# Hybrid decoder layer on one core: the sums of the down weights are issued from the second run of gate and up rows on

## The chip, the cores and the metric

The kernel runs on one core of one Trainium2 chip. The metric is the device time of one execution in microseconds (us). A core has five engines that run side by side, each with its own queue in a fixed order: TensorE (PE, matrix products; its weight loads are listed as PEld), VectorE (DVE), ScalarE (ACT), GpSimd (POOL) and SyncE (SP, which only issues transfers here). An instruction at the head of a queue that waits for something holds up everything behind it on that engine. Transfers are issued from SP, ACT and POOL and are carried by 16 DMA engines.

## The reference

One decoder layer on x (2048 x 1024, float32). Its first product is `proj = rms_norm(x, g) @ w_in`, split into u (512 columns, for the state-space branch), q, k and v. u goes through a diagonal state-space scan, a GELU and a gated product; q, k, v go through rotary embedding and attention over a window of 128 with sinks. Both branches are normed, joined and multiplied with w_out, normed and added to x. Then a SwiGLU feed-forward part follows: `gu = rms_norm(h) @ w_gate_up`, `ff = (silu(gate) * up) @ w_down` (2816 inner columns), normed and added.

```
def rms_norm(x, g):
    xf = x.astype(jnp.float32)
    y = xf * lax.rsqrt(jnp.mean(xf * xf, axis=-1, keepdims=True) + NORM_EPS)
    return (y * g.astype(jnp.float32)).astype(x.dtype)
```

## The kernel before, in words

Every float32 operand of a product is split into a high and a low part (line 166: a cast on ACT, a subtraction on DVE), and a product is three matmuls (lines 219 to 221). The 2048 rows are dealt with in four blocks of 512.

The first stage, `phase_proj`, weaves `u_stream` (the u products) with `table_stream` (tables for the state-space branch, mostly DVE work), and then the q, k, v products with the state-space scan. In `u_stream` the rows are not normed before the product. The product of a block is formed in four PSUM banks; beside it, x is loaded a second time in row layout (the tile `xn`, 512 KB each, four per block, two buffers), and ACT squares and sums it (`x_square`, line 344, into `ssq_x`). `rstd_block` then computes 1/sqrt for the block on POOL: `rsqrt`, lines 87 to 99, a chain of 15 tiny instructions on 128 x 4 numbers, each reading the one before. ACT writes the result into a diagonal matrix (`diag`, line 358), PE multiplies that with ones (`ps_bc`, line 360), ACT copies it out (`rstd_bc`, line 361), and DVE multiplies the block's four banks with it on their way out (`ust`, line 368). All four banks of one block have to be emptied that way before the next block's products can have them: `u_out` and the products of the next block both use the bank tag "pd", which has four.

The order of the instructions on each engine is not that of the program text. Up to the end of `phase_mix` a planner lays it out ahead of time: it goes through the program with its own reckoning of when each instruction's inputs are there and how long it will take, and gives an engine that it believes free the most urgent instruction that it believes ready. What it lays down is fixed in the queue; the chip follows that order whatever the real times are. The feed-forward part, `phase_ffn` (line 1355), stands under `manual_schedule`: there each engine keeps the order in which the program text issues its instructions. But that order only says which of them follows which. The first instruction of that part on an engine can still be laid down by the planner as early as its inputs are there, among the work of the earlier stages, and then the second one, until one comes whose input is made late.

In the feed-forward part `ffn_gu` (lines 1362 to 1399) runs over 21 runs of gate and up rows (`gu_runs`: run 0 holds rows 0 and 11, every further run one row block), each run in four quarters q. Between the products it does side work: `side` (the second half's channel transposes, q of 0 and 1), `pieces`, and `sums`. `sums` is `down_sums` (lines 1463 to 1478): 48 transfers from DRAM to DRAM, issued on POOL, that build four sums of halves of w_down in the DRAM tiles `ws_d` (`wsd` in the profile); the first 12 are plain copies out of w_down into two of the four. Each needs at most transfers issued 6 or 12 places before it. One is issued at q = 2, one at q = 3, and one at the end of each run (line 1395), so three a run, until the 48 are used up. At the end of every second run `ff_operands` (line 1448) issues three stores of the finished activations on POOL (`fxd`), which wait for DVE. `ffn_down` later reads `wsd` through SP.

Of the kernel before, what the change touches and what calls it, by code (L numbers as in the profile page):

```python
# [47 lines left out]
class Layer:  # L48
# [1313 lines left out]
    def ffn_gu(self, s):  # L1362
        nc, tc = self.nc, self.tc
        with ExitStack() as c:
            def right(name, bufs):
                return c.enter_context(tc.tile_pool(name=name, bufs=bufs, side="right", reuse_waits="tile"))

            ev, self.f_p[5] = right("f_ev", 1), right("f_p5", 1)
            ff, fc, self.f_p[6] = right("f_ff", 1), right("f_c", 1), right("f_p6", 1)
            pieces = self.act_steps(s, (5, 6), self.f_s, ("sa", "sa"))  # L1370
            pieces = [lambda: None] + pieces[:2] + [lambda: None] + pieces[2:]
            self.dn, self.dn_next = {}, 0
            sums = iter(()) if s else self.down_sums()
            side = [] if s else self.channel_steps(1, fc, "hx", 1, fc, "oo", 1, "pd")
            F4 = None
            for n, fs in enumerate(self.gu_runs()):
                if fs[0] < NJ:
                    j = fs[0]
                    F4 = ff.tile([P, 4, TB], F32, tag="f4", name=f"f4_{s}_{j}")
                groups = [self.gu_group(s, f, F4, ev) for f in fs]  # L1380
                for q in range(4):
                    for g in groups:
                        self.gu_ahead()
                        if fs[-1] == NF - 1 and q:
                            self.dn_ahead(s, q if q > 1 else 1)
                        next(g, None)
                        if pieces:
                            pieces.pop(0)()
                    if q > 1:
                        next(sums, None)  # L1390
                    elif side and n > 0:
                        side.pop(0)()
                if fs[-1] >= NJ:
                    self.ff_operands(s, j, F4)
                next(sums, None)
            for f in side:
                f()
            for _ in sums:
                pass
# [294 lines left out]
```

## Time and profile before

| | |
|---|---|
| time, median of 3 runs | 2166.42 us (2161.72 to 2170.81) |
| the profiled execution's own time | 2160.93 us |
| its span, first to last instruction | 2159.2 us |
| mean granted TensorE clock | 0.969 |
| busy: PE / DVE / ACT / POOL | 2001.8 / 1377.6 / 919.0 / 330.0 us |
| transfers from w_down or wsd into wsd | 48, of 512 KB or 256 KB |

Stages on PE by their first instruction in the trace: u products from 6.1 us, q, k and v products from 164.3, feed-forward products from 845.6 us, first read of `wsd` at 1323.3 us. A row of the timeline gives the start, the duration, the engine, the line, the operation and tiles, the number of instructions merged, and in brackets how long the engine stood idle before it and what ended that.

### The profile page before, as it was taken

How to read it: one execution, taken by the hardware profiler on the slowest of the kernel's cores; microseconds unless marked ns; L12 is line 12 of the kernel's file. 1: busy time of each engine (PE TensorE's matmuls, PEld its weight loads, DVE VectorE, ACT ScalarE, POOL GpSimd, SP SyncE). 2: the span in 40 equal slices, each digit the busy share in tenths (PEclk: the TensorE clock that was granted, in tenths of full speed). 3: DMA queues.
4: the chain of work that ended last, by engine and by line, in shares of the span. 5: the costliest groups of instructions: out<-in, count | busy, mean ns of one | idle time of the engine just before them, and what ended most of it. 6: DMA issues, size and time to landing. Idle time of an engine off the chain costs nothing.

```text
span 2159.2 us, 26000 instructions
## 1 busy us (share of the span) xinstructions
PE 2001.8 (93%) x9264; PEld 1630.3 (76%) x9264; DVE 1377.6 (64%) x2167; ACT 919.0 (43%) x1502; POOL 330.0 (15%) x667
## 2 busy tenths in 40 slices
PE   5499989889899889999999999999999999999995
PEld 3487656678787767788888888887788888888884
DVE  6548767698677676665566665557655565555447
ACT  5234211686576554533333334543433333334432
POOL 1301100021313342222122110005000000000003
PEclk8699999999999999999999999999999999999997
DMA  8246765733515683668588367766423232256655
GB/s 283 95 171 230 246 173 159 181 94 98 166 59 179 217 299 124 214 196 219 183 235 220 118 214 235 229 223 245 160 83 118 93 127 93 85 175 209 197 189 204
DMA packets 178003, 379.75 MB, mean 176 GB/s; under 512 B 32928, under 2 KB 53920, under 8 KB 177680
## 3 DMA queue, kind: packets, MB, share of 16 engines
q1 hardware_dynamic: 138400, 258.84, 37.5%
q0 software_dynamic: 32800, 110.84, 16.3%
q10 hardware_dynamic: 6672, 8.40, 1.2%
q8 instruction: 73, 1.20, 0.2%
q14 instruction: 58, 0.48, 0.1%
HBM read 281.87 MB, written 119.21 MB: 186 GB/s over the span
## 4 chain that ended last, share of the span: by engine, by line
PE 67%; DVE 8%; DMA 6%; issue 6%; POOL 3%; ACT 2%; SPq 0%; ACTq 0%; DVEq 0%; POOLq 0%
PE ps_gb L219 7%; PE ps_gb L220 7%; PE ps_gb L221 7%; PE ps_dn L220 6%; PE ps_dn L221 6%; PE ps_dn L219 6%; PE ps_gc L221 3%; PE ps_gc L219 3%; PE ps_gc L220 3%; PE ps_wo L219 2%; PE ps_wo L221 2%; PE ps_wo L220 2%; PE ps_ga L221 2%; PE ps_ga L219 2%; PE ps_ga L220 2%
## 5 line engine op out<-in xcount | busy, mean ns | idle before, releaser
L219 PE MATMUL ps_gb<-bh,wh 128*128 128x512 f32 x704 | 276.8, 393 | 6.4 <-ACT q L1420 6.1
L220 PE MATMUL ps_gb<-bl,wh 128*128 128x512 f32 x704 | 275.9, 392 | 0.0
L221 PE MATMUL ps_gb<-bh,wl 128*128 128x512 f32 x704 | 275.6, 391 | 0.0
L221 PE MATMUL ps_dn<-wh_w,wl_x 128*128 128x512 f32 x616 | 241.1, 391 | 4.4 <-DVE wl_x L171 4.4
L219 PE MATMUL ps_dn<-wh_w,wh_x 128*128 128x512 f32 x616 | 240.9, 391 | 0.6 <-ACT wh_x L170 0.5
L220 PE MATMUL ps_dn<-wl_w,wh_x 128*128 128x512 f32 x616 | 240.9, 391 | 0.0
L1330 ACT CAST wh<-gur 128x1024 fp32r<-128x1024 f32 x132 | 119.0, 902 | 182.8 <-DVE gur L75 175.1
L171 DVE TENSOR_TENSOR wl_x<-xr,wh_x 128x1024 fp32r<-128x1024 f32 x72 | 83.8, 1164 | 150.4 <-ACT wh_x L170 150.3
L75 DVE TENSOR_TENSOR wl<-gur,wh 128x1024 fp32r<-128x1024 f32 x132 | 139.5, 1057 | 50.6 <-ACT wh L1330 50.6
L219 PEld LDWEIGHTS ps_gb<-bh,wh 128*128 128x128 f32 x704 | 132.4, 188 | 37.8 <-ACT q L1420 7.7
L221 PEld LDWEIGHTS ps_gb<-bh,wl 128*128 128x128 f32 x704 | 132.4, 188 | 29.3
L220 PEld LDWEIGHTS ps_gb<-bl,wh 128*128 128x128 f32 x704 | 132.4, 188 | 28.9
L170 ACT CAST wh_x<-xr 128x1024 fp32r<-128x1024 f32 x72 | 70.8, 984 | 192.5 <-PE ps_dn L220 103.4
L220 PE MATMUL ps_gc<-bl,wh 128*128 128x512 f32 x352 | 137.9, 392 | 1.0 <-DVE bl L171 1.0
L221 PEld LDWEIGHTS ps_dn<-wh_w,wl_x 128*128 128x128 f32 x616 | 116.4, 189 | 29.4 <-DVE wl_x L171 5.3
L221 PE MATMUL ps_gc<-bh,wl 128*128 128x512 f32 x352 | 137.8, 392 | 0.0
L219 PE MATMUL ps_gc<-bh,wh 128*128 128x512 f32 x352 | 137.8, 392 | 0.0
L219 PEld LDWEIGHTS ps_dn<-wh_w,wh_x 128*128 128x128 f32 x616 | 116.4, 189 | 25.8 <-ACT wh_x L170 1.4
L220 PEld LDWEIGHTS ps_dn<-wl_w,wh_x 128*128 128x128 f32 x616 | 116.2, 189 | 24.1
L171 DVE TENSOR_TENSOR wl_w<-wr,wh_w 128x1024 fp32r<-128x1024 f32 x84 | 99.4, 1183 | 8.2 <-ACT wh_w L170 8.2
L1455 POOL DMA_DIRECT2D fxd<-f x22 | 17.1, 776 | 507.7 <-DVE f L75 463.9
L1428 ACT COPY u<-ps_gb 128x512 f32<-128x512 f32 x44 | 25.8, 587 | 142.1 <-PE ps_gb L221 142.1
(388 smaller groups left out, 4567.8 us busy)
## 6 DMA issues: line engine op xcount, KB each, us to landing
gur<-in_w_gu SPq DMA_DIRECT2D x88, 512.0 KB
xr<-fxd SPq DMA_DIRECT2D x70, 512.0 KB
wr<-wsd SPq DMA_DIRECT2D x40, 512.0 KB
fxd<-f POOLq DMA_DIRECT2D x22, 768.0 KB, 4.3
gwr_o<-in_w_out SPq DMA_DIRECT2D x64, 256.0 KB
wsd<-in_w_down POOLq DMA_DIRECT2D x30, 512.0 KB, 9.9
wr<-in_w_down SPq DMA_DIRECT2D x30, 512.0 KB
raw<-in_xT SPq DMA_DIRECT2D x56, 256.0 KB
```

Source lines behind the costliest of these rows:

```text
L75: (eng or self.nc.vector).tensor_tensor(out=out, in0=a, in1=b, op=op)
L170: nc.scalar.copy(hi, x)
L171: nc.vector.tensor_tensor(out=lo, in0=x, in1=f32(hi), op=ALU.subtract)
L219: t.matmul(out, wh, mh, start=first, stop=False, skip_group_check=more)
L220: t.matmul(out, wh, ml, start=False, stop=False, skip_group_check=more)
L221: t.matmul(out, wl, mh, start=False, stop=last, skip_group_check=more)
L1330: nc.scalar.copy(a[0], a[2])
L1428: nc.scalar.copy(u2, b)
L1455: nc.gpsimd.dma_start(to[0:3].rearrange("b p t -> p b t"), F4[:, 0:3])
```

## The change

In the first run (n = 0) the transfers at q = 2 and q = 3 are no longer issued. The one at the end of run 0 (line 1395) stays and is now the first; every later transfer moves two places back in the order in which the sums are issued. The number of transfers and what they move stay the same. With three a run and one in run 0, the last two of the 48 are now issued in run 16 instead of run 15.

```
                     if q > 1:
-                        next(sums, None)
+                        if n:
+                            next(sums, None)
                     elif side and n > 0:
                         side.pop(0)()
```

## Rows read from the trace of the kernel before

**Rows 1.** The page, busy tenths of PE in 40 equal slices of the span

```profile
PE   5499989889899889999999999999999999999995
```

**Rows 2.** Waits, 0 to 110 us: engine, tile, line, releaser, total us, times, longest

```profile
PE ps_bc L360 <- ACT diag L358: 43.9, 1, 43.9
...
POOL rsq_vd L87 <- ACT xn L344: 57.8, 4, 19.6
```

**Rows 3.** Timeline of POOL, 0 to 85 us, in the order of its queue

```profile
1.97 0.77 POOL L1477 DMA_DIRECT2D wsd<-in_w_down  x1
22.34 0.33 POOL L87 TENSOR_SCALAR rsq_vd<-ssq_x 128x4 f32<-128x4 f32 x1 [19.60 <-ACT xn L344]
34.96 0.20 POOL L87 TENSOR_SCALAR rsq_vd<-ssq_x 128x4 f32<-128x4 f32 x1 [12.29 <-ACT xn L344]
35.22 0.61 POOL L422 DMA_DIRECT2D cosd<-t_cs  x1
35.87 0.71 POOL L88 TENSOR_SCALAR rsq_hd<-rsq_vd 128x4 f32<-128x4 f32 x1
...
54.11 0.19 POOL L87 TENSOR_SCALAR rsq_vd<-ssq_x 128x4 f32<-128x4 f32 x1 [13.26 <-ACT xn L344]
...
69.38 0.61 POOL L87 TENSOR_SCALAR rsq_vd<-ssq_x 128x4 f32<-128x4 f32 x1 [12.67 <-ACT xn L344]
70.06 0.65 POOL L1477 DMA_DIRECT2D wsd<-in_w_down  x1
...
79.03 0.88 POOL L99 TENSOR_TENSOR rstd<-rsq_td,rsq_yd 128x4 f32<-128x4 f32 x2
...
81.18 0.35 POOL L92 TENSOR_TENSOR rsq_td<-rsq_yd 128x4 f32<-128x4 f32 x2
```

**Rows 4.** Timeline of all engines, 36 to 90 us

```profile
36.59 0.63 PE L221 MATMUL ps_u<-xs,wl 128*128 128x512 f32 x1
...
79.79 1.28 ACT L358 ACTIVATE diag<-ident,rstd 128x128 f32<-128x128 f32 x4 [10.49 <-POOL rstd L99]
...
81.12 2.07 PE L360 MATMUL ps_bc<-diag,ones 128*128 128x512 f32 x2 [43.91 <-ACT diag L358]
...
87.43 0.78 PE L219 MATMUL ps_u<-xs,wh 128*128 128x512 f32 x1
```

**Rows 5.** Stretches: us, busy of PE, PEld, DVE, ACT, POOL, PEclk, DMA, GB/s

```profile
0.00:37.00 37.00, 26.98 (x96) 19.41 (x96) 29.07 (x133) 22.42 (x38) 4.42 (x14) 0.96 0.85 290
37.00:81.00 44.00, 0.21 (x1) 0.00 (x0) 27.65 (x65) 15.26 (x30) 17.54 (x50) 0.54 0.58 196
81.00:92.00 11.00, 10.88 (x35) 8.88 (x36) 5.76 (x9) 2.42 (x7) 4.00 (x25) 0.51 0.00 0
92.00:155.00 63.00, 63.00 (x303) 51.72 (x302) 24.92 (x45) 18.91 (x43) 2.97 (x5) 1.00 0.36 130
155.00:400.00 245.00, 214.28 (x1044) 159.89 (x1043) 175.14 (x338) 70.95 (x162) 24.26 (x57) 0.97 0.67 200
```

**Rows 6.** Timeline of POOL, 872 to 880 us: one chain of 15, first and last

```profile
872.90 0.99 POOL L87 TENSOR_SCALAR rsq_vq<-ssq_h 128x4 f32<-128x4 f32 x1 [0.51 <-ACT junk_m L1066]
...
878.38 0.20 POOL L99 TENSOR_TENSOR rstd<-rsq_tq,rsq_yq 128x4 f32<-128x4 f32 x1
```

**Rows 7.** Timeline of POOL, 860 to 1500 us: first store of activations, last sums

```profile
893.32 0.85 POOL L1455 DMA_DIRECT2D fxd<-f  x1 [14.74 <-DVE f L75]
...
1167.72 3.63 POOL L1477 DMA_DIRECT2D wsd<-in_w_down  x4
```

**Rows 8.** Instructions that touch wsd: duration ns min/median/max, first and last start

```profile
L1223 SPq DMA_DIRECT2D wr<-wsd x48: 332/360/378, 1323.3 to 2081.5; - x48
```

**Rows 9.** Groups of DVE, 200 to 400 us: busy us, mean ns, idle before

```profile
L75 DVE TENSOR_TENSOR a<-ps_S,tab 128x512 f32<-128x512 f32 x32 | 21.2, 686 | 19.7 <-PE ps_S L654 19.7
L75 DVE TENSOR_TENSOR b<-z,tab 128x512 f32<-128x512 f32 x32 | 20.7, 688 | 0.3
L667 DVE TENSOR_TENSOR_SCAN z<-rho,a 128x256 f32<-128x256 f32 x32 | 20.3, 676 | 0.0
```

## The prediction

> **What bounds the kernel now.** I read the page's slices first. PE is busy nine tenths or more nearly everywhere, and the hole is at the start: 5 and 4 tenths in the first two slices of 54 us [rows 1]. So a change counts where it makes PE start sooner or wait less, and the first 108 us are where PE has most to gain. The waits of that stretch name the hole: one single wait of 43.9 us, of `ps_bc` for ACT's `diag` [rows 2]. The timeline shows its two ends: PE ends the first block's products at 36.59 + 0.63 = 37.22 us and starts `ps_bc` at 81.12 [rows 4]. ACT's `diag` started at 79.79, released by POOL's `rstd` [rows 4], so the cause lies on POOL.
>
> POOL's own queue tells the rest [rows 3]. The chain of the first block starts at 22.34, when that block's squares are summed. Its second step (line 88) needs nothing but the first, yet runs at 35.87. In front of it in the queue stands the first step of the second block's chain, which waits 12.29 us for that block's squares. Later the third block's first step holds POOL for 13.26 us and the fourth's for 12.67. Only then, behind a transfer into `wsd` at 70.06, does the first block's chain go on, to end at 79.03 + 0.88 = 79.91. The three foreign waits make 38.2 us of its 57.6 us. PE's hole is thus an order on POOL that doesn't fit the real times.
>
> Why that order? The two transfers into `wsd` at 1.97 and 70.06 belong to the feed-forward part; they are the two that run 0 issues at q = 2 and q = 3, laid down this early because they need nothing. On the chip POOL spends 0.77 and 0.65 us on them [rows 3]. The planner must have reckoned with far more. The second one needs nothing either and POOL stood idle for 19.60, 12.29, 13.26 and 12.67 us before it, yet it was laid down behind all four first steps. That fits only if the planner believed POOL to be occupied by the first transfer until the inputs of both the first and the second chain were there (in truth 12.6 us apart), then gave POOL the backlog most urgent first, and put in the second transfer when it saw nothing ready. `cosd` supports it, an unrelated store that went out right behind the second chain's first step. This is an inference from the order; no row states what the planner believed.
>
> **What the change does, step by step.** (a) The two transfers leave the start. The first POOL instruction of the feed-forward part is now the store `fxd`, which waits for DVE and runs at 893.32 [rows 7]; nothing of that part can be laid down on POOL before its input is made. The planner then lays out POOL's first 100 us without the two. I expect the first chain to go down in one piece, behind its own squares and before the second chain's first step.
>
> (b) The new end of the hole. The chain starts at 22.34 as now. Undisturbed, 15 steps took from 872.90 to 878.58, 5.7 us [rows 6]; beside a busy DVE the last pair of steps took 0.88 us and the undisturbed pair 0.35 [rows 3], so up to 2.5 times as long, 14.3 us. `rstd` is ready between 28.0 and 36.6. From 79.91 to `ps_bc` at 81.12 it was 1.2 us. That makes 29 to 38 us, and PE is busy with the first block until 37.2. So nearly the whole wait of 43.9 us can go: minus 43.1 to minus 43.9. I take 43.9.
>
> The Trainium skill, "SBUF — State Buffer", section "Who interferes with whom", says that a DVE instruction with two SBUF inputs and a GpSimd instruction that reads SBUF exclude each other for a whole instruction. The pairs of 0.88 and 0.35 us agree with that in direction. If each of the 15 steps lost one 0.69 us DVE instruction, the chain would take 16 us and end at 38.4, and the gain would be 41.5 in place of 43.9. The sum below doesn't use this.
>
> (c) What is late next. The queues of PE and ACT are in order too. If the planner believes the chain shorter than it is, it lays `diag` and `ps_bc` among the last products and casts of the first block, and these wait. Price: from none to the chain's full length, 14 us; the undisturbed chain's half is the nearest guess, plus 3.
>
> (d) The clock. After the hole the granted clock was 0.51 for 11 us [rows 5], near the lower level of 1.2 GHz; 35 matmuls took 10.88 us there and 303 took 63.0 afterwards, so 0.31 against 0.21 us each, 3.6 us lost. It was falling already before the hole, with PE poorly fed. Between none and minus 3.6; I take minus 1.8.
>
> (e) The loads of the start. One 512 KB transfer less while the DMA engines are 0.85 busy at 290 GB/s [rows 5]: 0.52 MB / 290 GB/s is up to 1.8 us; loads here partly wait for buffers, so minus 0.5. At 70.06 nothing on PE waited for data.
>
> (f) Given back later. DVE did 27.65 us of work under the hole [rows 5], mostly tables. It now lies beside the next blocks' products, where DVE is busy 24.92 of 63 us: 38 us are free, room for all. Behind that, 155 to 400 us, PE is busy 214 and DVE 175 of 245 [rows 5], and the order is laid out anew there as well. If all of the tables' work came onto the path, plus 27.7; if the new order closed all of PE's gaps, minus 30.7. The cover I see is nearly enough, so I take plus 5.
>
> (g) The feed-forward part. Each sum moves two places on POOL. The last four started at 1167.72 to 1171 [rows 7]; two of them go into the next run, some 20 us later. The first read of `wsd` is at 1323.3 [rows 8], so over 130 us cover it, and the stores between them move by at most two issues of about 1 us. Nothing; without that cover each late sum would hold PE about as long as a transfer takes.
>
> Sum: minus 43.9, plus 3, minus 1.8, minus 0.5, plus 5, is minus 38.2 us. The profiled execution took 2160.93 us (span 2159.2 and 1.7 around it), so 2122.7 on its scale. The median of the runs is 2166.42, 5.5 above that execution; on that scale 2128.2, and I predict 2128. From the start of the u products' second block on all is bound by PE and by order, nothing by absolute time, so what is won there should reach the end.
>
> **Rivals.** (1) The order stays as it is: the planner had another reason to lay the first steps ahead, for instance that it believes the squares of all blocks to come close together. Then only the transfers' own time goes: 0.65 us off the chain and up to 1.8 of (e), so 2164 to 2166. For it: the pair of chains at 81.18 also runs in lockstep [rows 3]. Against it: the second transfer's place, which that does not explain.
>
> (2) The hole goes and about half is given back in the state-space stage: DVE holds the a, z and b steps there, 62.2 us of busy time with 19.7 us of waits for PE [rows 9], and tables that come later than u would stretch it. Terms (c) and (f) at 14 and 12 then leave about minus 20: 2146.
>
> (3) Slower than before. The planner, with u early, lays the q products ahead of the state-space products, because the tables can't come sooner. The a, z, b steps then no longer lie beside q products. Place: 200 to 400 us. Price: up to 62.2 us uncovered [rows 9] plus the 14 of (c), against a gain of about 46 from (b), (d) and (e); it decides from 46 us on, and the whole of it gives 2166.4 - 46 + 76 = 2196. For it: DVE is at 175 of 245 us there. Against it: the u products of three more blocks take over 60 us first, time for the tables.
>
> **How the numbers follow.** The forecast (25 to 50 us gained, 2116 to 2141) has 0.68, rival 2 0.12, rival 1 0.11, rival 3 0.09. About 0.5% (11 us) is what a measurement of this kernel can tell from no change. Faster by more than that: the forecast and nearly all of rival 2, 0.79. Within it: rival 1 and a rest, 0.12. Slower: rival 3, 0.09. Low end: terms (b), (d), (e) in full, 49 us, and 10 of the 30.7 that a better order could win in (f): 2108. High end: rival 2 with a little more given back, 2158, short of rivals 1 and 3, which hold 0.2.
>
> **What would show it.** In the profile after: no `wsd` row on POOL before the first `fxd`; POOL's first chain without a foreign wait inside, ending before 40 us; `ps_bc` before 45 us with a wait under 10 us; the second slice of PE at 8 or 9 tenths; the feed-forward part starting about 38 us earlier; its length unchanged. (f) is wrong if the stretch from the last u product to the first gate product is longer than before by more than 10 us. The prediction fails if `ps_bc` still waits for the fourth block's squares.

## The result, and the profile after

The changed kernel takes 2127.17 us (median of 4 runs, 2126.79 to 2128.03), the kernel before beside it 2164.76 (4 runs). The ratio is 0.9824, 95% interval 0.9801 to 0.9846: 37.6 us less, against 38.2 predicted. The profiled execution took 2126.79 us with a span of 2124.9, 34.3 less than the span before. In the repeat further down the gain is 40.8 us (2127.76 against 2168.56 of 9 runs of the kernel before). So the 38.2 is met within some 3 us, and the closer agreement here is luck.

The hole at the start is gone. The page of the changed kernel, busy tenths of PE, beside [rows 1]:

```profile
PE   7999798999898899999999999998999999999995
```

The cause is to be seen on POOL's queue (timeline of the changed kernel, 0 to 80 us, beside [rows 3]):

```profile
22.26 0.32 POOL L87 TENSOR_SCALAR rsq_vd<-ssq_x 128x4 f32<-128x4 f32 x1 [20.21 <-ACT xn L344]
22.66 0.25 POOL L88 TENSOR_SCALAR rsq_hd<-rsq_vd 128x4 f32<-128x4 f32 x1
...
27.52 0.20 POOL L99 TENSOR_TENSOR rstd<-rsq_td,rsq_yd 128x4 f32<-128x4 f32 x1
...
28.53 0.56 POOL L422 DMA_DIRECT2D cosd<-t_cs  x1
...
36.45 0.19 POOL L87 TENSOR_SCALAR rsq_vd<-ssq_x 128x4 f32<-128x4 f32 x1 [4.86 <-ACT xn L344]
...
57.15 0.19 POOL L87 TENSOR_SCALAR rsq_vd<-ssq_x 128x4 f32<-128x4 f32 x1
```

There is no `wsd` row left (the first is at 863.1). The second step of the first chain, at 22.66, stands right behind the first; before, the second block's first step stood between them. `rstd` is ready at 27.72 in place of 79.91. The waits of 0 to 110 us (columns as in [rows 2]) and the first `ps_bc`:

```profile
ACT diag L358 <- POOL rstd L99: 16.2, 4, 7.1
...
PE ps_u L219 <- ACT xs L170: 11.7, 4, 6.0
...
PE ps_bc L360 <- ACT diag L358: 0.2, 1, 0.2
```

```profile
29.08 1.13 PE L360 MATMUL ps_bc<-diag,ones 128*128 128x512 f32 x2 [0.20 <-ACT diag L358]
```

So 43.9 us of wait became 0.2. Where the rest of the time stands is read by stages. The last u product starts at 164.0 us before and at 125.8 after, the last score product (`ps_sc`) at 702.2 and 664.2, the first gate product (`ps_gb`) at 845.6 and 812.7. The stretches (columns as in [rows 5]), of the kernel before:

```profile
37.00:164.00 127.00, 83.09 (x376) 68.07 (x376) 64.65 (x127) 41.11 (x91) 26.86 (x83) 0.80 0.44 153
164.00:702.20 538.20, 484.64 (x2582) 389.78 (x2581) 397.79 (x762) 281.05 (x572) 87.29 (x220) 0.97 0.54 158
702.20:845.60 143.40, 127.75 (x607) 104.21 (x606) 94.13 (x142) 74.35 (x122) 48.78 (x108) 0.95 0.68 226
```

of the changed kernel:

```profile
0.00:37.00 37.00, 26.97 (x102) 19.64 (x102) 29.84 (x126) 22.92 (x41) 9.41 (x34) 1.00 0.81 276
37.00:125.80 88.80, 83.34 (x371) 67.53 (x371) 61.79 (x134) 38.74 (x89) 22.83 (x60) 0.92 0.64 212
125.80:664.20 538.40, 484.90 (x2582) 391.22 (x2580) 398.49 (x762) 281.30 (x571) 87.46 (x220) 0.96 0.53 158
664.20:812.70 148.50, 132.97 (x608) 108.75 (x607) 94.52 (x142) 74.49 (x122) 49.30 (x108) 0.92 0.65 218
```

The u stage gained 38.2 us (164.0 to 125.8). The state-space and score stages took the same, 538.2 and 538.4. The stretch behind them took 5.1 more, the feed-forward part 1.4 less (1313.6 and 1312.2). The sum is minus 34.3.

### The profile page after: what moved, and what is told of

The parts are those of the page before. It is cut to its first block, busy times and chain, and to the rows that moved or that the text cites. A ratio compares the mean times of both kernels' runs of the same rounds, so it can differ in the third digit from the quotient of the medians.

```text
span 2124.9 us, 25992 instructions
## 1 busy us (share of the span) xinstructions
PE 2006.2 (94%) x9264; PEld 1635.4 (77%) x9264; DVE 1375.8 (65%) x2167; ACT 917.6 (43%) x1502; POOL 331.9 (16%) x667
## 4 chain that ended last, share of the span: by engine, by line
PE 69%; DVE 8%; issue 6%; DMA 5%; POOL 3%; ACT 2%; SPq 0%; ACTq 0%; DVEq 0%; POOLq 0%
PE ps_gb L219 7%; PE ps_gb L220 7%; PE ps_gb L221 7%; PE ps_dn L221 6%; PE ps_dn L219 6%; PE ps_dn L220 6%; PE ps_gc L221 4%; PE ps_gc L220 4%; PE ps_gc L219 4%; PE ps_wo L219 2%; PE ps_wo L221 2%; PE ps_wo L220 2%; PE ps_ga L220 2%; PE ps_ga L219 2%; PE ps_ga L221 2%
```

## The experiments

The theory: the two early transfers cost through the place that they push the first reciprocal-root chain to, and the planner does that because it believes a transfer to hold the issuing engine for long. The rivals: the transfers cost by themselves (POOL's time, load on the DMA engines); only the second one, ahead of the chain's rest, does the harm; any early instruction does it, whatever it moves.

**One transfer left at the start.**

```diff
-                        if n:
+                        if n or q == 2:
                             next(sums, None)
```

> The changed kernel, but of the two transfers of run 0 the first (at q = 2) is issued there again; only the second stays away. Nothing of the computation is left out. Order theory (the transfers cost through the place that they push the first block's reciprocal-root chain to, not through their own time): one transfer at the head of POOL's queue is enough to split the first chain, so ps_bc again waits about 43 us for diag, and the time is 2160 to 2166. Rival, transfers that cost by themselves, each the same: half of the 37.6 us comes back, about 2146, with a wait of about 22 us. Rival, only the second transfer (the one at 70.06 ahead of the chain's rest) does the harm: about 2127, and no wait above 10 us.

Measured 2166.34 us (10 runs) against 2167.44 of before, ratio 0.9999 (0.9989 to 1.0009). One transfer does all of the harm, and it is the first. POOL's timeline shows the split of before, with no second `wsd`:

```profile
1.98 0.76 POOL L1478 DMA_DIRECT2D wsd<-in_w_down  x1
21.87 0.22 POOL L87 TENSOR_SCALAR rsq_vd<-ssq_x 128x4 f32<-128x4 f32 x1 [19.14 <-ACT xn L344]
35.47 0.28 POOL L87 TENSOR_SCALAR rsq_vd<-ssq_x 128x4 f32<-128x4 f32 x1 [13.38 <-ACT xn L344]
...
53.81 0.19 POOL L87 TENSOR_SCALAR rsq_vd<-ssq_x 128x4 f32<-128x4 f32 x1 [13.08 <-ACT xn L344]
...
68.64 0.19 POOL L87 TENSOR_SCALAR rsq_vd<-ssq_x 128x4 f32<-128x4 f32 x1 [12.23 <-ACT xn L344]
```

```profile
78.68 2.07 PE L360 MATMUL ps_bc<-diag,ones 128*128 128x512 f32 x2 [42.90 <-ACT diag L358]
```

**Both transfers kept, the chains on DVE.**

```diff
-        self.rsqrt(self.rstd1[:, sl], self.ssq_x[:, sl], D, 4)
+        self.rsqrt(self.rstd1[:, sl], self.ssq_x[:, sl], D, 4, eng=nc.vector)
```

> The kernel before, with both transfers at POOL's start as they were, but the reciprocal-root chains of the input's rows (rstd1) computed on DVE in place of POOL. Nothing of the computation is left out. Order theory: what the transfers hold up on POOL is no longer on the path, so the wait of 43.9 us goes with the transfers still there: 2122 to 2135. Rival, the transfers' own cost (their 1.4 us on POOL, their load on the DMA engines at the start, or anything else that goes with their being early): the time stays at 2160 to 2167. Rival, the chain on DVE gets behind the tables there: the wait is shortened in part only, 2140 to 2155.

Measured 2127.61 us, ratio 0.9821 (0.9798 to 0.9843): the whole gain with both transfers where they were. The first rows are POOL's, the last is PE's, which waits for nothing there:

```profile
1.97 0.75 POOL L1477 DMA_DIRECT2D wsd<-in_w_down  x1
...
70.51 0.57 POOL L1477 DMA_DIRECT2D wsd<-in_w_down  x1
```

```profile
37.12 1.02 PE L360 MATMUL ps_bc<-diag,ones 128*128 128x512 f32 x2
```

The same chains on DVE without the two early transfers took 2126.31 us (further down). So neither the DMA load of the early transfers nor their time on POOL cost anything that can be measured. It was what stood behind them in POOL's queue.

**The transfers early on ACT's queue.**

```diff
         L.setup()
+        for jp in range(2):
+            tc.nc.scalar.dma_start(L.ws_d[1][jp][0:2],
+                                   I["w_down"][2 * jp:2 * jp + 2, :, 512:1024])
...
+                if dst == S1 and op is None and jp < 2:
+                    continue
```

> The changed kernel, but the two transfers that it took from the start are issued there all the same, from ACT's queue right behind the setup, so that the DMA engines carry the same 1 MB early and POOL carries none of it. The sum is the same. Order theory: POOL's first chain stays in one piece, ps_bc starts before 40 us, and the time is that of the changed kernel, 2126 to 2133 (up to 2 us for the DMA time and two issues on ACT). Rival, the early load is what cost the time: 2155 to 2166.

A miss: 2168.01 us (10 runs), ratio 1.0006 (0.9988 to 1.0024), just above the 2155 to 2166 that the load rival gave. But the trace shows another cause. Rows of DVE and of PE:

```profile
51.13 1.29 DVE L171 TENSOR_TENSOR xs<-raw,xs 128x512 fp32r<-128x512 f32 x2
```

```profile
13.43 0.80 PE L219 MATMUL ps_u<-xs,wh 128*128 128x512 f32 x1 [13.43 <-ACT wh L173]
51.87 0.79 PE L220 MATMUL ps_u<-xs,wh 128*128 128x512 f32 x1 [37.65 <-DVE xs L171]
```

DVE's very first `xs` was laid behind its table steps and ran at 51.13, though ACT's cast for it began at 5.80 and took 0.62 us; in the changed kernel the first one ran at 6.15. With no `xs` done, no buffer came free: SP waited 38.5 us for it with the next loads, and the DMA engines were 0.05 busy from 17 to 50 us. So the transfers made a hole of like size (37.65 us) in another place. That is how the theory's mechanism would look with ACT as the engine believed to be held. As a test of the load this kernel was no good, since it changed the order as well. The kernel above is the test of the load, and the one with small pieces on ACT tests this reading.

**Smaller pieces at POOL's start.** The kernel before, but each of the first two sums moves 8 of its 128 rows, in the second kernel 32; the rest of both follows with the third sum.

```diff
+        late = []
...
+                if dst == S1 and op is None and jp < 2:
+                    late.append((y[:, 8:], x[:, 8:]))
+                    y, x = y[:, 0:8], x[:, 0:8]
+                else:
+                    while late:
+                        nc.gpsimd.dma_start(*late.pop(0))
```

> The kernel before, with both sums issued in run 0 as there, but each of these two first moves only 8 of its 128 rows (32 KB in place of 512); the rest of both follows with the third sum. The sums are the same. The theory that the planner lays POOL's queue out by the length that it believes a transfer to have: two short ones don't hold POOL in its plan, so the first chain stays whole, ps_bc waits under 1 us, and the time is that of the changed kernel, 2125 to 2131, though the two transfers still stand at the head of POOL's queue. Rival, any transfer that is free to go at the start splits the chain: the hole of about 43 us stays, 2160 to 2167.

> As the kernel with 8 rows, but 32 of the 128 rows of each (128 KB). Place theory: the queue then has the second block's first step in front of the first block's second, and the fourth block's first step in front of the first chain's end, so a quarter of the bytes costs the whole hole: ps_bc again waits about 43 us, 2160 to 2167. Rival, cost in proportion to the bytes moved early: a quarter of 37.6 us, about 2137.

With 8 rows 2127.52 us, ratio 0.9818 (0.9794 to 0.9841); with 32 rows 2160.47, ratio 0.9958 (0.9942 to 0.9974). POOL's timeline with 8 rows:

```profile
1.97 1.40 POOL L1484 DMA_DIRECT2D wsd<-in_w_down  x2
21.52 0.44 POOL L87 TENSOR_SCALAR rsq_vd<-ssq_x 128x4 f32<-128x4 f32 x1 [18.14 <-ACT xn L344]
22.04 0.66 POOL L88 TENSOR_SCALAR rsq_hd<-rsq_vd 128x4 f32<-128x4 f32 x1
...
27.66 0.24 POOL L99 TENSOR_TENSOR rstd<-rsq_td,rsq_yd 128x4 f32<-128x4 f32 x1
```

and with 32:

```profile
1.97 0.89 POOL L1484 DMA_DIRECT2D wsd<-in_w_down  x1
22.81 0.19 POOL L87 TENSOR_SCALAR rsq_vd<-ssq_x 128x4 f32<-128x4 f32 x1 [19.95 <-ACT xn L344]
35.85 0.19 POOL L87 TENSOR_SCALAR rsq_vd<-ssq_x 128x4 f32<-128x4 f32 x1 [12.85 <-ACT xn L344]
...
43.84 1.74 POOL L1484 DMA_DIRECT2D wsd<-in_w_down  x1
...
74.44 0.75 POOL L99 TENSOR_TENSOR rstd<-rsq_td,rsq_yd 128x4 f32<-128x4 f32 x2
```

At the head of the queue the real issue takes POOL 0.70, 0.89 and 0.77 us with 8, 32 and 128 rows, nearly the same. Yet the first size leaves the chain whole and the other two split it. Against the kernel with 8 rows, 32 rows cost 33.0 us (`ps_bc` waits 39.4) and 128 rows, the kernel before, 41.0 us (2168.56 beside them); in proportion to the bytes 32 rows would cost about 10. The order is laid down before anything runs, and it changes with the size while the real issue hardly does: the second transfer goes out directly behind the first with 8 rows, at 43.84 us with 32 and at 70.06 with 128. That fits a planner that gives a longer transfer a longer stay on POOL. Its estimate itself was not read out in any run.

**Small pieces on ACT's queue.** As the kernel with the transfers on ACT, with 8 rows each; the other 120 rows of both go out on POOL with the first sums of the feed-forward part.

```diff
+        for jp in range(2):
+            tc.nc.scalar.dma_start(L.ws_d[1][jp][0:2, 0:8],
+                                   I["w_down"][2 * jp:2 * jp + 2, 0:8, 512:1024])
...
+                if dst == S1 and op is None and jp < 2:
+                    y, x = y[:, 8:], x[:, 8:]
```

> As the kernel that issues the two transfers early on ACT's queue, but each moves only 8 of its 128 rows there (32 KB in place of 512); the rest follows in the second run, on POOL. The sums are the same. In the kernel with the whole transfers on ACT the hole came up in another place: DVE's first xs stood behind some 100 table steps, ran at 51 us, and PE stood still for 37.7 us. If the believed length of the transfers on ACT made that order, short ones should bring DVE's xs forward to some 10 to 15 us (it stands behind some 30 short table steps in its queue) and PE should wait under 12 us there: 2130 to 2142. Rival, any instruction ahead on ACT's queue makes it, whatever it moves: 2160 to 2170, with xs at 50 us again.

Measured 2139.75 us, ratio 0.9860 (0.9841 to 0.9880), as expected. DVE's first `xs` came forward from 51.13 to 10.93. PE's first three waits are 8.91, 1.97 and 7.35 us, where the whole transfers made 13.43 and 37.65. The last u product starts at 137.1 us, 11.3 after that of the changed kernel, about the 12.6 us by which this kernel is slower. So even short pieces are not free on ACT.

**The sums from the sixth run on.** The transfers at q = 2 and q = 3 begin with the sixth run; the one at the end of each run stays, so the later ones move eight places further back.

```diff
-                        if n:
+                        if n > 4:
                             next(sums, None)
```

> The changed kernel with the sums issued from the sixth run of gate and up rows on in place of the second. Nothing is left out. By the prediction's step on the feed-forward part, over 130 us lie between the last sum and its first read, so the sums can come four runs later still at no cost: 2125 to 2130, no change against the changed kernel. Rival, the sums are near their deadline: the first down products wait for them, and the time is 5 us or more above the changed kernel, 2132 or more.

Measured 2129.31 us, ratio 0.9828 (0.9809 to 0.9848), not to be told from the changed kernel. Instructions that touch `wsd`, of the changed kernel (columns as in [rows 8]):

```profile
L1223 SPq DMA_DIRECT2D wr<-wsd x48: 332/360/540, 1289.7 to 2047.5; - x48
L1478 POOL DMA_DIRECT2D wsd<-in_w_down x36: 559/1054/1977, 863.1 to 1161.9; - x36
```

and with the sixth run:

```profile
L1223 SPq DMA_DIRECT2D wr<-wsd x48: 332/359/585, 1296.4 to 2054.4; - x48
L1478 POOL DMA_DIRECT2D wsd<-in_w_down x36: 555/1034/1960, 869.9 to 1226.6; - x36
```

From the start of the last sum to the first read 127.8 us are left in the changed kernel and 69.8 here; the cover is real.

**The changed kernel again, and with the chains on DVE.** The second has the edit of the kernel above with the chains on DVE.

> The changed kernel once more, for a second profile. In the first, 5 of the 38 us won at the start were given back from the last score product to the first gate product, with the same instructions and the same waits, where the granted clock read 0.50 for some 6 us. If this belongs to the new order, it recurs here (148 to 151 us for that stretch, 2127 in all); if it is a chance of the run, the stretch takes 143 to 145 and the profiled run is some 5 us shorter, about 2120.

> The changed kernel with the reciprocal-root chains of the input's rows on DVE in place of POOL. Nothing is left out. A try at a version faster than both: with the transfers at the start this brought the u products to an end at 118 us in place of 126, but the state-space products came no earlier for it. Expected 2120 to 2128; rival, the chains delay the tables on DVE and it is slower than the changed kernel, 2130 to 2136.

The repeat measured 2127.76 us, ratio 0.9813 (0.9792 to 0.9833); its profiled span is 2120.5. The chains on DVE gave 2126.31, ratio 0.9815 (0.9795 to 0.9835): no difference, so no version here beats the changed kernel. Stretches of the repeat:

```profile
0.00:37.00 37.00, 28.63 (x102) 21.97 (x103) 29.70 (x126) 23.41 (x41) 11.62 (x42) 0.95 0.84 282
37.00:120.60 83.60, 78.85 (x371) 63.54 (x370) 61.65 (x134) 38.41 (x87) 21.05 (x53) 0.98 0.64 222
120.60:660.50 539.90, 485.08 (x2582) 390.97 (x2582) 397.93 (x762) 280.79 (x572) 87.20 (x220) 0.96 0.53 158
660.50:807.90 147.40, 128.40 (x607) 104.09 (x606) 94.50 (x142) 74.24 (x122) 48.99 (x108) 0.95 0.65 220
```

The expectation on the last stretch came out between its two ends: 147.4 us, but with PE busy 128.40 and not 132.97.

## Why the prediction was right

The terms, against the two profiles of the changed kernel. PE's idle time up to the last u product was 164.0 - 26.98 - 83.09 = 53.9 us before [rows 5], and 125.8 - 26.97 - 83.34 = 15.5 and 120.6 - 28.63 - 78.85 = 13.1 after; the hole's wait is taken out of it for (c).

| step | predicted | first profile | second |
|---|---|---|---|
| (b) wait of `ps_bc` | -43.9 | -43.7 | -43.9 |
| (c) other idle time of PE up to the last u product | +3 | +5.3 | +3.1 |
| (d) PE's busy time up to there | -1.8 | +0.2 | -2.6 |
| (e) loads of the start | -0.5 | in (c) | in (c) |
| (f) last u to last score product | +5, from 155 to 400 us | +0.2 | +1.7 |
| last score to first gate product | none | +5.1 | +4.0 |
| (g) feed-forward part | 0 | -1.4 | -1.0 |
| sum | -38.2 | -34.3 | -38.7 |

**(a) and (b)** held as put. The inference on the planner, which no row could show, is borne out by the three sizes, though its estimate was never seen. Its reading of the second transfer fits too: the first alone splits the chain, and the second goes out directly behind the first when both are short. The chain took 27.72 - 22.26 = 5.5 us beside a DVE that was busy 7.59 of 8 us from 20 to 28 us, so the low end of the 5.7 to 14.3 was right. The Trainium skill, "SBUF — State Buffer", section "Who interferes with whom", has a DVE instruction with two SBUF inputs contend with a GpSimd instruction that reads SBUF. The trace agrees in direction: two large DVE instructions ran beside the chain (128x512, from 25.38 to 26.74), and the two steps beside them took 0.56 and 0.52 us, where the other 13 took 0.20 to 0.32. The 16 us that the prediction worked out didn't come about, since the rest of DVE's work there was small.

**(c)** has the right sign and size, and its place in part. `ps_bc` at 29.08 lies between products of the first block, ACT's `diag` waits for `rstd` four times (16.2 us), and PE's waits for ACT's `xs` grew from 8.3 to 11.7 us, but only to 8.9 in the repeat. Waits that (c) doesn't name are new: `ps_krev`, a product for the tables, waits 2.4 us in the first profile and 3.8 in the repeat.

**(d)** depends on the run. Over the same 371 matmuls PE was busy 83.34 us at a mean granted clock of 0.92 in one profile and 78.85 at 0.98 in the other. The fall behind the hole is gone, but the clock now falls in other places, in the first profile to 0.57 from 84 to 92 us, behind that wait of 2.4 us.

**(e)** is too small to be seen; both transfers stood in their early places in the kernel with the chains on DVE, with no loss that can be measured (2127.61 us, and 2126.31 without them).

**(f)** is the step whose cause and place failed; its size fitted by luck. By the sign that the prediction set, more than 10 us longer from the last u product to the first gate product, it passes: 686.9 us against 681.6. But the tables' work that lay under the hole cost nothing here: DVE was busy 61.79 of the 88.8 us beside the products, and the stretch from 125.8 to 664.2 is as long as before. (It isn't so in every kernel: with the transfers kept and the chains on DVE, the last u product starts at 118.3 us and the last score product still at 664.4; why stays open.) What was given back came some 550 us later, where PE runs the same instructions in the same order. In the first profile it is the clock. The kernel before in three slices of 4 us, and the changed kernel at the same instructions:

```profile
710.20:714.20 4.00, 2.38 (x20) 1.95 (x19) 1.70 (x4) 4.00 (x8) 0.70 (x1) 1.00 0.58 185
714.20:718.20 4.00, 4.00 (x28) 3.56 (x28) 1.99 (x7) 1.27 (x3) 0.71 (x1) 1.00 0.64 197
718.20:722.20 4.00, 4.00 (x25) 3.44 (x24) 1.91 (x4) 2.91 (x5) 0.00 (x0) 1.00 0.18 65
```

```profile
672.20:676.20 4.00, 2.30 (x17) 1.86 (x16) 1.65 (x4) 4.00 (x8) 0.65 (x1) 0.93 0.50 175
676.20:680.20 4.00, 4.00 (x16) 3.71 (x16) 1.46 (x6) 0.16 (x1) 0.77 (x2) 0.50 0.64 197
680.20:684.20 4.00, 4.00 (x18) 3.40 (x18) 1.38 (x2) 1.57 (x3) 0.00 (x0) 0.72 0.00 0
```

Nearly the same gap in PE's work (`ps_O` waits 1.62 and 1.70 us for DVE's `ho`) is followed by full clock in the one and by 0.50, the level of 1.2 GHz, in the other; 34 matmuls in 8 us in place of 53. Over the whole stretch it makes 132.97 - 127.75 = 5.2 us of busy time. It doesn't belong to the order alone: the stretch took 148.5 and 147.4 us in the changed kernel, 150.6 with the sums from the sixth run on, 150.8 with its chains on DVE and 147.6 with small pieces on ACT, but 144.6 with 8 rows on POOL, 144.6 with the transfers kept and the chains on DVE, and 143.4 to 144.7 in the four kernels with a long hole at the start. In the repeat the clock held at that gap, and 3.3 us more of idle PE took its place. What decides it is open; the measured medians contain it.

**(g)** held. The last sum came 25 us later, counted from the first gate product (349.2 after it in place of 324.0), as put, and its cover was there with 70 us to spare when the sums came later still. Of the signs that the prediction named, one came out short in the first profile: the feed-forward part started 32.9 us earlier in place of about 38 (37.7 in the repeat).

**The rivals.** Rival 1 is refuted by the result. Rivals 2 and 3 put their price in the state-space stage, which took 538.4 us against 538.2.

## What to carry to other kernels

When an instruction that needs nothing is written far ahead of its use, look where the planner lays it, and at what it then lays behind it on the same engine: the price here was 38 us of order for 0.7 us of real issue. The sign is a chain that is split by another chain's first step, with that engine idle in between for data. Moving such a transfer to another engine can move the hole with it, as ACT's queue did here. Issue it behind something that holds it back. Short pieces were free on POOL, but cost 12 us on ACT.

## What the runs showed of the hardware

At the head of its queue the issue of a transfer from DRAM to DRAM took POOL 0.70, 0.89 and 0.77 us for 32, 128 and 512 KB, so the size doesn't show there; elsewhere in the queue of the kernel before such issues took 0.49 to 1.88 us. The granted clock fell after a gap of 1.70 us and not after one of 1.62 with the same instructions around it, worth 5 us of 149 in one stretch; two profiles of one kernel differed by 4.4 us of span. A stage's gain of a few us can't be read from one profile.
